# Attention with keys on the partitions, its denominators summed on GpSimd, beside a recurrence whose chunks come first in each step

## The chip, the cores and the metric

The kernel runs on one core of a Trainium2 chip. The metric is the device time of one execution in microseconds; three runs of the kernel before gave 4550.06, 4560.07 and 4565.6, so the median is 4560.07.

## The reference

Two layers of a diffusion transformer on 1024 latent and 256 context tokens of width 1024, all in fp32. In each layer a mixer runs two things side by side: an RWKV-7 recurrence in two directions (8 heads of 64) and an attention (8 heads, queries and keys of 96, values of 64). Latent queries see all 1280 keys, context queries the 256 context keys (first layer only). Input projections come before the mixer, an output projection and a gated FFN with a convolution behind it.

```python
def attend(q, k, v):
    s = jnp.einsum('bqhd,bkhd->bhqk', q, k).astype(F32) * (QK_DIM ** -0.5)
    p = jax.nn.softmax(s, axis=-1).astype(v.dtype)
    return jnp.einsum('bhqk,bkhd->bqhd', p, v)
...
    def step(s, inp):
        r_t, w_t, k_t, v_t, kk_t, a_t = inp
        sa = jnp.einsum('bhvk,bhk->bhv', s, kk_t)
        s = (s * w_t[:, :, None, :]
             - sa[..., None] * (kk_t * a_t)[:, :, None, :]
             + v_t[..., None] * k_t[:, :, None, :])
        return s, jnp.einsum('bhvk,bhk->bhv', s, r_t)
```

## The kernel before

The program is a sequence of stages: input projection (`in_proj`), mixer, output projection (`out_proj`), FFN, once for each layer. A scheduler in the tile framework orders the instructions of each engine from the order of the code and a model of its own, so neighbouring pieces of code end up interleaved on the in-order engines. DMAs are all issued by SyncE (SP).

**Mixer** (`mixer`, L758). Ten steps `i`, each of 128 tokens in each direction. Per step the recurrence has two chunks (`rwkv_seq`, L957: products, the copies `Z` and `W`, then the new state, one half of which is multiplied on VectorE and one on GpSimd, L999, and `S` on GpSimd, L1001); `rwkv_inv2` (L935) ends the inverse of step `i+1`; `rwkv_prep` (L840) prepares step `i+2` and calls `rwkv_inv` (L902). There a loop of 31 turns (L925, L926) solves sixteen small triangular systems with 62 dependent VectorE instructions, each with both inputs in SBUF; it is called **the chain** here. There are 20 chains, ten in each layer. Its tile `T` is set up on GpSimd (L917, L919), and its result is transposed on VectorE into `X` by four instructions (L932). In the code of a step the attention of that step comes first, then the two chunks.

**Attention** (`attn`, L1037), one call for a pair of heads and 128 queries, 72 calls in all (64 latent, 8 context). Queries are on the partitions: three matmuls for each key segment (high and low parts of a split in two, L1075) give scores in three PSUM tiles `sp`; VectorE takes the least of each (L1076) and joins them (L1085); ScalarE makes `exp(least - score)` and its row sums (L1088); VectorE joins the sums (L1095) and inverts them (L1096). Then 128x128 pieces of `P` are transposed on TensorE (L1107), copied out of PSUM by VectorE and ScalarE in turn (L1110, L1112) and multiplied by the values (L1117). The inverse sums are spread over partitions by a product with the identity (L1120), copied (L1122) and multiplied in (L1123).

**Behind the mixer.** When the last inverse is done, its SBUF is given to the output projection's weights: `split_wo` (L748) loads 16 pieces of 256 KB into a tile `raw` with two buffers, and splits each on ScalarE (L755) and VectorE (L756). The first products of `out_proj` are those of L1228.

```python
for j in range(31):
    r, w = 31 - j, j // 2 + 1
    tmp = p.tile([128, 152], F32, name="tmp", tag="tmp")
    tv = tmp[:, :r * w].rearrange("p (a b) -> p a b", b=w)
    eng.tensor_tensor(tv, bc(Dt[:, j + 1:, j:j + 1], [128, r, w]), bc(T[:, j:j + 1, :w], [128, r, w]), op=ALU.mult)
    eng.tensor_tensor(T[:, j + 1:, :w], T[:, j + 1:, :w], tv, op=ALU.subtract)
```

Of the kernel before, what the change touches and what calls it, by code (L numbers as in the profile page):

```python
# [22 lines left out]
NP = 4  # L23
# [8 lines left out]
CUTS = [(0,), (1,), (2,)]  # L32
# [41 lines left out]
def bc(ap, shape):  # L74
    return ap.to_broadcast(shape)
# [6 lines left out]
class Kern:  # L82
# [654 lines left out]
    def load_wo(self, l, st):  # L737

        nc = self.nc
        wp = st.enter_context(self.tc.tile_pool(name=f"ow{l}", bufs=1, side="right", reuse_waits="tile"))  # L740
        self.wo = [None] * 8
        for k in range(7, -1, -1):
            self.wo[k] = [wp.tile([128, D], F32R, name=f"{nm}{k}") for nm in ("lo", "hi")][::-1]
        with self.tc.tile_pool(name=f"or{l}", bufs=2, side="right", reuse_waits="tile") as p:
            for k in range(8):
                self.split_wo(l, k, p, "raw")
# [11 lines left out]
    def mixer(self, l, wst):  # L758
        tc = self.tc
        with ExitStack() as st:  # L760
# [6 lines left out]
            order = ([8, 9] if need_ctx else []) + [3, 4, 2, 5, 1, 6, 0, 7]  # L767
            work = [(h, t) for h in range(NP) for t in order]
# [4 lines left out]
            for i in range(10):  # L773

                upto = len(work) * (i + 1) // 10 if i < 9 else len(work)
                for h, t in work[done:upto]:
                    self.attn(l, h, t, t == order[0])
                done = upto
                self.rwkv_seq(l, i, 0)
                self.rwkv_seq(l, i, 1)  # L780
# [121 lines left out]
    def rwkv_inv(self, l, i, AB):  # L902
# [26 lines left out]
        X = R.X[i % 2]  # L929
        for j in range(4):  # L930
            r = slice(32 * j, 32 * j + 32)
            nc.vector.transpose(X[r, :, 32 * (j % 2):32 * (j % 2) + 32], TD[r])  # L932
        R.inv = (AB, TD)

    def rwkv_inv2(self, l, i):  # L935
# [19 lines left out]
        nc.vector.tensor_copy(X[64:96, :, 32:64], ps[64:96])  # L955

    def rwkv_seq(self, l, i, c):  # L957
# [21 lines left out]
        nc.vector.tensor_copy(Z, ps)  # L979
# [49 lines left out]
    def attn_setup(self, l, st):  # L1029
        tc = self.tc  # L1030
        A = self.A = Ctx()
        A.n = 0
        A.p = st.enter_context(tc.tile_pool(name=f"A{l}", bufs=1, reuse_waits="tile"))
        A.ps = st.enter_context(tc.tile_pool(name=f"As{l}", bufs=1, space=PSUM, reuse_waits="tile"))
        A.pp = st.enter_context(tc.tile_pool(name=f"Ap{l}", bufs=1, space=PSUM, reuse_waits="tile"))

    def attn(self, l, h, t, first):  # L1037

        nc = self.nc
        A = self.A  # L1040
        p = A.p
        if first:
            A.k = []
            for e in range(2):
                raw = p.tile([128, NTOK], F32, name="raw", tag="P", bufs=3)[0:96]
                nc.sync.dma_start(out=raw[0:64], in_=self.kD[l][2 * h + e])
                nc.sync.dma_start(out=raw[64:96], in_=self.krD[l])
                k = p.tile([96, 2, NTOK], F32R, name="ka", tag=f"ka{e}")
                nc.scalar.activation(k[:, 0], raw, AF.Copy)
                nc.vector.tensor_tensor(k[:, 1], raw, k[:, 0], op=ALU.subtract)  # L1050
                A.k.append(k)
            A.v = p.tile([128, NTOK // 128, 128], F32, name="va", tag="va")
            nc.sync.dma_start(out=A.v, in_=self.vD[l][:, :, h * 128:(h + 1) * 128].rearrange("t p x -> p t x"))
        raw = p.tile([96, 2, 128], F32, name="qr", tag="qr", bufs=2)
        nc.sync.dma_start(out=raw, in_=self.qD[l][2 * h:2 * h + 2, :, t * 128:(t + 1) * 128].rearrange("h r t -> r h t"))
        q = p.tile([96, 2, 2, 128], F32R, name="qa", tag="qa", bufs=2)
        nc.scalar.activation(q[:, 0], raw, AF.Copy)
        nc.gpsimd.tensor_tensor(q[:, 1], raw, q[:, 0], op=ALU.subtract)
        key_segs = SEGS if t < 8 else SEGS[2:]
        k0 = key_segs[0][0]  # L1060
        nk = NTOK - k0
        Ps, dn = [], []
        for e in range(2):
            mx = p.tile([128, 12], F32, name="mx", tag="mx", bufs=6)
            P = p.tile([128, NTOK], F32, name="P", tag="P", bufs=3)
            cut = CUTS if t < 8 else [(2,)]
            sps = []
            for i, c in enumerate(cut):
                sp = A.ps.tile([128, 512 * max(len(x) for x in CUTS[i:i + 1])], F32, name="sp", tag=f"s{i}")
                b0 = SEGS[c[0]][0]  # L1070
                w = sum(SEGS[x][1] for x in c)
                for x in c:
                    o, n = SEGS[x]
                    for m, (qq, kk) in enumerate(((0, 0), (0, 1), (1, 0))):
                        nc.tensor.matmul(sp[:, o - b0:o - b0 + n], q[:, qq, e], A.k[e][:, kk, o:o + n], start=m == 0, stop=m == 2)  # L1075
                nc.vector.tensor_reduce(mx[:, i:i + 1], sp[:, :w], axis=AX.X, op=ALU.min)  # L1076
                sps.append((sp, b0 - k0, w))
            nx = len(cut)
            mn = mx[:, 0:1]
            if nx > 1:  # L1080
                mn = mx[:, 8:9]
                if nx == 2:
                    nc.vector.tensor_tensor(mn, mx[:, 0:1], mx[:, 1:2], op=ALU.min)
                else:
                    nc.vector.tensor_reduce(mn, mx[:, 0:nx], axis=AX.X, op=ALU.min)  # L1085

            for i, (sp, o, w) in enumerate(sps):
                nc.scalar.activation(P[:, o:o + w], sp[:, :w], AF.Exp, bias=mn, scale=-1.0, accum_out=mx[:, 4 + i:5 + i])  # L1088
            sm = mx[:, 4:5]
            if nx > 1:  # L1090
                sm = mx[:, 9:10]
                if nx == 2:
                    nc.vector.tensor_tensor(sm, mx[:, 4:5], mx[:, 5:6], op=ALU.add)
                else:
                    nc.vector.tensor_reduce(sm, mx[:, 4:4 + nx], axis=AX.X, op=ALU.add)  # L1095
            nc.vector.reciprocal(mx[:, 3:4], sm)  # L1096
            Ps.append(P)
            dn.append(mx[:, 3:4])
        av = A.pp.tile([128, 512], F32, name="av", tag="av")
        half = [slice(0, 64), slice(64, 128)]  # L1100
        nkt = nk // 128
        for kp in range(nkt // 2):
            tp = A.pp.tile([128, 2, 2, 128], F32, name="tp", tag="tp", bufs=1)
            for e in range(2):
                for b in range(2):
                    o = (kp * 2 + b) * 128
                    nc.tensor.transpose(tp[:, b, e], Ps[e][:, o:o + 128], self.ident)  # L1107
            pT = p.tile([128, 2, 2, 128], F32, name="pT", tag="pT", bufs=2)
            if A.n % 2:
                nc.scalar.activation(pT, tp, AF.Copy)  # L1110
            else:
                nc.vector.tensor_copy(pT, tp)  # L1112
            A.n += 1
            for b in range(2):
                kt = kp * 2 + b
                for e in range(2):
                    nc.tensor.matmul(av[half[e], 0:128], A.v[:, k0 // 128 + kt, half[e]], pT[:, b, e], start=kt == 0, stop=kt == nkt - 1)  # L1117

        for e in range(2):
            nc.tensor.matmul(av[half[e], 128:256], bc(dn[e], [128, 64]), self.ident, start=True, stop=True)  # L1120
        o1 = p.tile([128, 128], F32, name="o1", tag="o1", bufs=2)
# [346 lines left out]
```

## Time and profile before

| | |
|---|---|
| median of three runs | 4560.07 us |
| profiled execution | 4568.71 us, span 4566.9 us |
| TensorE busy | 4159.5 us (91%) |
| VectorE busy | 2736.5 us (60%) |
| ScalarE busy | 1688.5 us (37%) |
| GpSimd busy | 541.9 us (12%) |
| granted TensorE clock | 0.938 of full speed |

The profiled execution is 8.6 us above the median. Busy shares are means over stages with different limits: the mixers run from about 690 to 1420 us and from about 3018 to 3705 us of the span, and what the change touches is almost all in there. The busy time of an engine is the union of its instructions' records; TensorE's records overlap each other, because matmuls are pipelined.

### The profile page before, as it was taken

The page shows a single profiled execution, that of the slowest core. Times are in us where ns is not written, and L with a number is a line of the kernel's source. Part 1 is how long each engine was busy: PE and PEld are TensorE (multiplying, and loading weights), DVE is VectorE, ACT ScalarE, POOL GpSimd, SP SyncE. Part 2 cuts the span into 40 slices and gives each one's busy share as a digit, 9 for nine tenths or more (in the row PEclk, how much of TensorE's full clock was granted, in tenths as well). Part 3 has the DMA queues.
Part 4 walks back from the last instruction along what each step waited for, and adds up shares of the span by engine and source line. Part 5 has one row for each costly group of instructions (what it writes and reads, how often), then busy time and mean ns, then how long its engine had stood idle before and what let it go on. Part 6 is the DMA issues. An engine that isn't in the chain of part 4 may idle for free. (4 is left out here: it accounts for less than half of the span.)

```text
span 4566.9 us, 72983 instructions
## 1 busy us (share of the span) xinstructions
PE 4159.5 (91%) x29598; PEld 3294.7 (72%) x29598; DVE 2736.5 (60%) x4943; ACT 1688.5 (37%) x3000; POOL 541.9 (12%) x492
## 2 busy tenths in 40 slices
PE   8978888888888899999998989988889878999998
PEld 5756656676766788888886866666777666888887
DVE  3225567888885534554447235569887866555456
ACT  3213455444554432221224224454445534222222
POOL 1000000111222300000004000001111244000002
PEclk9998889899998999999998998989998989999999
DMA  6652234323324211111113222343232243111111
GB/s 222 237 180 91 104 120 125 84 69 81 79 61 140 100 37 35 40 42 33 47 35 111 84 71 100 117 144 77 61 81 66 65 136 126 54 51 51 44 50 65
DMA packets 425698, 401.36 MB, mean 88 GB/s; under 512 B 243473, under 2 KB 329937, under 8 KB 425361
## 3 DMA queue, kind: packets, MB, share of 16 engines
q1 hardware_dynamic: 425360, 396.69, 28.1%
q8 instruction: 233, 3.82, 0.3%
q14 instruction: 105, 0.85, 0.1%
HBM read 285.85 MB, written 110.72 MB: 87 GB/s over the span
## 5 line engine op out<-in xcount | busy, mean ns | idle before, releaser
L1279 PE MATMUL up<-u,hi 128*128 128x512 f32 (+1 forms) x3520 | 1012.6, 369 | 4.2 <-ACT hi L1269 4.2
L1279 PEld LDWEIGHTS up<-u,hi 128*128 128x128 f32 x3520 | 643.8, 189 | 119.8 <-ACT hi L1269 4.6
L1279 PE MATMUL up<-u,lo 128*128 128x512 f32 (+1 forms) x1760 | 648.5, 368 | 0.0
L304 PE MATMUL pj<-u,whi 128*128 128x512 f32 (+1 forms) x1888 | 567.2, 385 | 36.0 <-DVE o L325 31.0
L1326 DVE TENSOR_TENSOR acc<-dn,acc 128x512 f32<-128x512 f32 x340 | 233.3, 688 | 432.9 <-PE dn L1320 432.8
L304 PEld LDWEIGHTS pj<-u,whi 128*128 128x128 f32 x1888 | 352.6, 198 | 139.4 <-issue 45.2
L1279 PEld LDWEIGHTS up<-u,lo 128*128 128x128 f32 x1760 | 332.1, 189 | 57.9 <-DVE lo L1271 0.3
L304 PE MATMUL pj<-u,wlo 128*128 128x512 f32 (+1 forms) x944 | 360.0, 382 | 0.1
L1075 PE MATMUL sp<-ka,qa 96*128 96x512 f32 (+1 forms) x1200 | 320.8, 399 | 37.2 <-ACT P L1088 26.1
L1269 ACT ACTIVATE hi<-raw 128x512 fp32r<-128x512 f32 x176 | 110.5, 630 | 564.4 <-PE up L1279 561.4
L1320 PE MATMUL dn<-hi,fh 128*128 128x512 f32 x792 | 311.8, 394 | 7.9 <-ACT fh L1294 4.0
L1320 PE MATMUL dn<-lo,fh 128*128 128x512 f32 x792 | 310.0, 391 | 0.0
L1320 PE MATMUL dn<-hi,fl 128*128 128x512 f32 x792 | 305.9, 390 | 0.0
L1088 ACT ACTIVATE P<-sp,mx 128x512 f32<-128x512 f32 (+1 forms) x400 | 240.0, 607 | 174.1 <-DVE mx L1085 98.4
L1117 PE MATMUL av<-pT,va 128*64 128x128 f32 x2624 | 235.5, 302 | 51.3 <-DVE pT L1112 25.5
L1075 PEld LDWEIGHTS sp<-ka,qa 96*128 96x128 f32 x1200 | 214.8, 205 | 89.6 <-ACT P L1088 38.5
L1107 PE MATMUL tp<-cst,P 128*128 128x128 f32 x1312 | 236.7, 303 | 22.5 <-ACT P L1088 16.4
L1076 DVE TENSOR_REDUCE mx<-sp 128x1 f32<-128x512 f32 (+1 forms) x400 | 229.4, 586 | 39.7 <-PE sp L1075 37.1
L1117 PEld LDWEIGHTS av<-pT,va 128*64 128x64 f32 x2624 | 152.0, 146 | 108.6 <-DVE pT L1112 31.7
L1271 DVE TENSOR_TENSOR lo<-raw,hi 128x512 fp32r<-128x512 f32 x176 | 125.4, 715 | 173.8 <-ACT hi L1269 161.3
L287 ACT ACTIVATE whi<-raw 128x512 fp32r<-128x512 f32 (+2 forms) x110 | 66.1, 602 | 435.7 <-PE pj L304 384.5
L304 PEld LDWEIGHTS pj<-u,wlo 128*128 128x128 f32 x944 | 186.6, 198 | 39.2 <-issue 7.3
(254 smaller groups left out, 7233.5 us busy)
## 6 DMA issues: line engine op xcount, KB each, us to landing
wt<-in_w_ada_dram SPq DMA_DIRECT2D x96, 512.0 KB
raw<-in_w_up_dram SPq DMA_DIRECT2D x176, 256.0 KB
raw<-in_w_down_dram SPq DMA_DIRECT2D x88, 256.0 KB
raw<-in_w_in_dram SPq DMA_DIRECT2D x84, 256.0 KB
bkD<-lt SPq DMA_DIRECT2D x32, 640.0 KB
BK<-bkD SPq DMA_DIRECT2D x320, 64.0 KB
KR<-kkD SPq DMA_DIRECT2D x152, 128.0 KB
kkD<-kx SPq DMA_DIRECT2D x16, 640.0 KB
```

What stands on the lines that cost most here:

```text
L287: nc.scalar.activation(hi[:, :m], raw[:, :m], AF.Copy)
L304: nc.tensor.matmul(ps[:, o:o + n], ww, u[k][s], start=k == 0 and j == 0, stop=k == nk - 1 and j == 2)
L1075: nc.tensor.matmul(sp[:, o - b0:o - b0 + n], q[:, qq, e], A.k[e][:, kk, o:o + n], start=m == 0, stop=m == 2)
L1076: nc.vector.tensor_reduce(mx[:, i:i + 1], sp[:, :w], axis=AX.X, op=ALU.min)
L1088: nc.scalar.activation(P[:, o:o + w], sp[:, :w], AF.Exp, bias=mn, scale=-1.0, accum_out=mx[:, 4 + i:5 + i])
L1107: nc.tensor.transpose(tp[:, b, e], Ps[e][:, o:o + 128], self.ident)
L1117: nc.tensor.matmul(av[half[e], 0:128], A.v[:, k0 // 128 + kt, half[e]], pT[:, b, e], start=kt == 0, stop=kt == nkt - 1)
L1269: nc.scalar.activation(hi, raw, AF.Copy)
L1271: nc.vector.tensor_tensor(lo, raw, hi, op=ALU.subtract)
L1279: nc.tensor.matmul(ps[:, so:so + sn], ww, uu[k][s], start=k == 0 and m == 0, stop=k == 7 and m == 2)
L1320: nc.tensor.matmul(ps, x[:, t * 128:(t + 1) * 128], w, start=m == 0, stop=m == 3 * len(js) - 1)
L1326: nc.vector.tensor_tensor(dst, ps, dst, op=ALU.add)
```

## The change

Attention is written anew, and four pieces around it are moved.

- A call now takes a pair of heads and 256 queries (36 units: 32 latent, 4 context). First, ahead of its use, the least score of each query is found from the high parts alone: one matmul where the scores take three (`least`), reduced on VectorE. Four small products put these on a row, which ScalarE copies into row 96 of the queries (`row`); row 96 of the keys is -1, so that the scores come out with the least already taken off.
- Scores have the keys on the partitions, 128 keys by 2 heads by 256 queries, six matmuls. ScalarE makes the exponentials straight into the form in which the products with the values need them: no transposes, no copies.
- GpSimd sums the exponentials over the ten key tiles (nine additions of 128x512 for a unit; 292 in all). At the end a product with ones sums over the partitions, and VectorE inverts 128x256 sums and multiplies.
- A unit is cut into steps of two key tiles; the steps of a layer are shared out among the ten steps of the mixer, and in the code each chunk of the recurrence comes before its half of the attention's steps.
- `X` comes from one transpose of 128x512 on VectorE and four copies on ScalarE; the copies `Z` and the second half of L954/L955 go to ScalarE.
- `raw` of the output projection's weights has one buffer in place of two; a scratch tile of `out_proj` is wider.

```diff
-        with self.tc.tile_pool(name=f"or{l}", bufs=2, side="right", reuse_waits="tile") as p:
+        with self.tc.tile_pool(name=f"or{l}", bufs=1, side="right", reuse_waits="tile") as p:
...
-                for h, t in work[done:upto]:
-                    self.attn(l, h, t, t == order[0])
+                self.rwkv_seq(l, i, 0)
+                for step in work[done:(done + upto) // 2]:
+                    step()
+                self.rwkv_seq(l, i, 1)
+                for step in work[(done + upto) // 2:upto]:
+                    step()
                 done = upto
-                self.rwkv_seq(l, i, 0)
-                self.rwkv_seq(l, i, 1)
...
+        Xt = p.tile([128, 16, 32], F32, name="Xt", tag="Xt")
+        nc.vector.transpose(Xt.rearrange("p u s -> p (u s)"), TD.rearrange("p u s -> p (u s)"))
         for j in range(4):
             r = slice(32 * j, 32 * j + 32)
-            nc.vector.transpose(X[r, :, 32 * (j % 2):32 * (j % 2) + 32], TD[r])
+            nc.scalar.activation(X[r, :, 32 * (j % 2):32 * (j % 2) + 32], Xt[r], AF.Copy)
...
-        nc.vector.tensor_copy(X[64:96, :, 32:64], ps[64:96])
+        nc.scalar.activation(X[64:96, :, 32:64], ps[64:96], AF.Copy)
...
-        nc.vector.tensor_copy(Z, ps)
+        nc.scalar.activation(Z, ps, AF.Copy)
...
+        def least(t):
...
+            def product(out, e, o, n):
+                nc.tensor.matmul(out, q[0:96, 0, e, tok], A.k[e][0:96, 0, o:o + n], start=True, stop=True)
...
+                for e in range(2):
+                    for i in range(2):
+                        sp = pp.tile([128, 512], F32, name="sp", tag="s", bufs=4)
+                        product(sp, e, 512 * i, 512)
+                        nc.vector.tensor_reduce(mx[:, e, i:i + 1], sp, axis=AX.X, op=ALU.min)
...
+        def scores(kt):
+            q = c["q"]
+            st = pp.tile([128, 2, 256], F32, name="st", tag="s", bufs=4)
+            ks = slice(kt * 128, (kt + 1) * 128)
             for e in range(2):
...
+                k = A.k[e]
+                nc.tensor.matmul(st[:, e], k[0:97, 0, ks], q[0:97, 0, e], start=True, stop=False)
+                nc.tensor.matmul(st[:, e], k[0:96, 0, ks], q[0:96, 1, e], start=False, stop=False)
+                nc.tensor.matmul(st[:, e], k[0:96, 1, ks], q[0:96, 0, e], start=False, stop=True)
+
+            P = c[kt] = p.tile([128, 2, 256], F32, name="P", tag="P", bufs=6)
+            nc.scalar.activation(P, st, AF.Exp, scale=-1.0)
+            if kt == kts[1]:
+                c["sum"] = p.tile([128, 2, 256], F32, name="Ps", tag="Ps")
+                nc.gpsimd.tensor_tensor(c["sum"], c[kts[0]], P, op=ALU.add)
+            elif kt > kts[1]:
+                nc.gpsimd.tensor_tensor(c["sum"], c["sum"], P, op=ALU.add)
...
+                nc.tensor.matmul(c["av"][half[e], 0], A.v[:, kt, half[e]], c[kt][:, e], start=kt == kts[0], stop=kt == kts[-1])
+
+        def close():
+
+            av = c["av"]
+            ones = bc(self.cst[:, CO_ONE:CO_ONE + 1], [128, 64])
+            for e in range(2):
+                nc.tensor.matmul(av[half[e], 1], ones, c["sum"][:, e], start=True, stop=True)
...
+            nc.vector.reciprocal(of, av[:, 1])
+            nc.vector.tensor_tensor(of, av[:, 0], of, op=ALU.mult)
...
+        def tiles(i):
+            for kt in kts[2 * i:2 * i + 2]:
+                scores(kt)
+            for kt in kts[2 * i - 2:2 * i] if i else []:
+                values(kt)
+            if 2 * i == len(kts):
+                close()
```

How the built programs stand. First VectorE in the first layer, where the fifth chain ends (`T` is the chain's tile, `Dt` its matrix; `KR` and `GA` belong to the preparation of the step after the next). Before, then after:

```order
L1123 TENSOR_TENSOR o_8939<-av,o_8939 128x128
L1112 COPY pT<-tp 128x512
L925 TENSOR_TENSOR tmp<-Dt,T 128x30
L1076 TENSOR_REDUCE mx<-sp 128x1
L926 TENSOR_TENSOR T<-T,tmp 128x2x15
L887 TENSOR_TENSOR KR<-g,cst 64x4x64
L890 TENSOR_TENSOR GA<-g,cst 128x256
L1085 TENSOR_REDUCE mx<-mx 128x1
L925 TENSOR_TENSOR tmp<-Dt,T 128x16
L926 TENSOR_TENSOR T<-T,tmp 128x16
L928 STREAM_TRANSPOSE TD<-T 128x32x16
L932 STREAM_TRANSPOSE X_4537<-TD 32x16x32 x4
```

```order
L925 TENSOR_TENSOR tmp_7517<-Dt_7427,T_7429 128x45
L926 TENSOR_TENSOR T_7429<-T_7429,tmp_7517 128x3x15
L925 TENSOR_TENSOR tmp_7520<-Dt_7427,T_7429 128x30
L926 TENSOR_TENSOR T_7429<-T_7429,tmp_7520 128x2x15
L925 TENSOR_TENSOR tmp_7523<-Dt_7427,T_7429 128x16
L887 TENSOR_TENSOR KR_8131<-g_8150,cst_60 64x4x64
L890 TENSOR_TENSOR GA_8148<-g_8150,cst_60 128x256
L926 TENSOR_TENSOR T_7429<-T_7429,tmp_7523 128x16
L887 TENSOR_TENSOR KR_8131<-g_8151,cst_60 64x4x64
L890 TENSOR_TENSOR GA_8148<-g_8151,cst_60 128x256
L928 STREAM_TRANSPOSE TD_7526<-T_7429 128x32x16
L931 STREAM_TRANSPOSE Xt_7528<-TD_7526 128x512
```

Between the turns of the chain stood pieces of the attention at nearly every place; now its last turns follow each other, with only the preparation between them, and one transpose of 512 columns stands for four.

Then GpSimd from the setting up of `T` for the fifth chain on, in the first layer (`W` and `S` are the recurrence's, `qa` the low parts of the queries, `Ps` the attention's sums). Before, then after:

```order
L917 MEMSET T_7651 128x512
L919 TENSOR_SCALAR T_7651<-cst_60 128x16 x2
L1058 TENSOR_TENSOR qa_8945<-qr_8943,qa_8945 96x256
L999 TENSOR_TENSOR W_6642<-St_8261,pc0_91 64x512
L1001 TENSOR_TENSOR S_8265<-St_8261,pc0_91 128x512
L1058 TENSOR_TENSOR qa_9058<-qr_9056,qa_9058 96x256
```

```order
L917 MEMSET T 128x512
L919 TENSOR_SCALAR T<-cst 128x16 x2
L1137 TENSOR_TENSOR Ps<-Ps,P 128x512 x4
L1135 TENSOR_TENSOR Ps<-P 128x512
L1137 TENSOR_TENSOR Ps<-Ps,P 128x512 x4
L1001 TENSOR_TENSOR W<-St,pc_91 64x512
L1003 TENSOR_TENSOR S<-St,pc_91 128x512
L1137 TENSOR_TENSOR Ps<-Ps,P 128x512 x4
```

The queue that held a handful of the recurrence's instructions for each step now holds the attention's sums between them, nine ahead of the first `W`.

Last ScalarE at the end of the first mixer, where the output projection's weights begin (`hi` are their high parts). Before, then after:

```order
L954 ACTIVATE X_4538<-p_13070 32x16x32
L755 ACTIVATE hi_13124<-raw 128x512 x2
L1110 ACTIVATE pT<-tp 128x512
L755 ACTIVATE hi_13122<-raw 128x512 x2
L985 ACTIVATE W<-q 64x512
L1088 ACTIVATE P,mx<-sp,mx 128x512 x2
```

```order
L956 ACTIVATE X_4539<-p_12269 32x16x32
L957 ACTIVATE X_4539<-p_12269 32x16x32
L754 ACTIVATE hi_12323<-raw 128x512
L981 ACTIVATE Z<-q 128x512
L754 ACTIVATE hi_12323<-raw 128x512
L987 ACTIVATE W<-q 64x512
```

The attention's exponentials, which went on beside the weights before, are all ahead of them now; beside the weights only the recurrence's last chunks are left.

## Rows read from the trace of the kernel before

**Rows 1.** Windows (us; busy of PE, PEld, DVE, ACT, POOL; clock, DMA): mixers, steady stretches.

```profile
690.00:1420.00 730.00, 629.04 (x8079) 493.93 (x8078) 584.03 (x1528) 376.38 (x872) 123.57 (x139) 0.92 0.33 86
3018.00:3705.00 687.00, 595.30 (x7636) 469.74 (x7634) 555.78 (x1460) 342.73 (x799) 110.70 (x125) 0.91 0.31 78
...
786.40:1347.10 560.70, 490.96 (x6808) 388.70 (x6807) 478.32 (x1268) 284.02 (x663) 103.32 (x116) 0.94 0.30 74
3098.30:3640.00 541.70, 478.05 (x6490) 378.95 (x6490) 466.47 (x1239) 266.10 (x621) 92.15 (x105) 0.93 0.28 70
```

**Rows 2.** TensorE in order of time, 1101 to 1103 us: start, length, what.

```profile
1101.81 0.66 PE L1117 MATMUL av<-pT,va 128*64 128x128 f32 x8
1102.30 0.39 PE L1120 MATMUL av<-cst,mx 128*64 128x128 f32 x4
1102.61 0.66 PE L1107 MATMUL tp<-cst,P 128*128 128x128 f32 x4
1103.03 0.95 PE L1075 MATMUL sp<-ka,qa 96*128 96x512 f32 x3
```

**Rows 3.** VectorE, then GpSimd, in order of time inside the tenth chain.

```profile
1311.10 0.68 DVE L996 TENSOR_TENSOR St<-q,S 128x512 f32<-128x512 f32 x1
1311.70 0.27 DVE L925 TENSOR_TENSOR tmp<-Dt,T 128x115 f32<-128x115 f32 x1
...
1313.44 1.11 DVE L926 TENSOR_TENSOR T<-T,tmp 128x115 f32<-128x115 f32 x1
...
1313.05 1.37 POOL L1001 TENSOR_TENSOR S<-St,pc 128x512 f32<-128x512 f32 x1
```

**Rows 4.** Groups by line and form, VectorE: count, busy us, mean ns, idle before.

```profile
L1076 DVE TENSOR_REDUCE mx<-sp 128x1 f32<-128x512 f32 x256 | 174.0, 683 | 37.8 <-PE sp L1075 35.5
L1076 DVE TENSOR_REDUCE mx<-sp 128x1 f32<-128x256 f32 x144 | 59.6, 414 | 1.9 <-PE sp L1075 1.6
L1112 DVE COPY pT<-tp 128x512 f32<-128x512 f32 x164 | 112.1, 684 | 29.0 <-PE tp L1107 27.6
L1085 DVE TENSOR_REDUCE mx<-mx 128x1 f32<-128x3 f32 x128 | 18.9, 148 | 0.8
L1096 DVE RECIPROCAL mx<-mx 128x1 f32<-128x1 f32 x144 | 22.2, 154 | 4.1 <-ACT P L1088 3.3
L1123 DVE TENSOR_TENSOR o<-av,o 128x128 f32<-128x128 f32 x72 | 20.2, 281 | 12.1 <-ACT o L1122 11.6 <-DMA BK<-bkD 0.3
L932 DVE STREAM_TRANSPOSE X<-TD 32x512 f32<-32x512 f32 x80 | 56.1, 701 | 1.1
L620 DVE TENSOR_TENSOR_SCAN lt<-rst,lt 128x640 f32<-128x640 f32 x32 | 45.9, 1475 | 11.5 <-issue 9.8 <-ACT lt L618 1.7
```

**Rows 5.** Groups by line: the chain's two lines, and a GpSimd addition of 128x512.

```profile
L926 DVE TENSOR_TENSOR T<-T,tmp 128x126 f32<-128x126 f32 (+22 forms) x620 | 198.2, 320 | 10.9
L925 DVE TENSOR_TENSOR tmp<-Dt,T 128x126 f32<-128x126 f32 (+22 forms) x620 | 185.1, 299 | 10.1
L834 POOL TENSOR_TENSOR ysb<-ysb,bo 128x512 f32<-128x512 f32 x18 | 23.0, 1277 | 110.7 <-DVE ysb L833 87.3 <-DVE mx L1096 16.1 <-DVE T L926 7.3
```

**Rows 6.** The chain's lines by themselves: least, median and longest ns, first and last start.

```profile
L925 DVE TENSOR_TENSOR tmp<-Dt,T x620: 154/264/1244, 745.8 to 3637.3; 128x126 f32<-128x126 f32 x15, 128x30 f32<-128x30 f32 x10, 128x78 f32<-128x78 f32 x10, 128x110 f32<-128x110 f32 x10
L926 DVE TENSOR_TENSOR T<-T,tmp x620: 147/267/1823, 746.5 to 3639.8; 128x126 f32<-128x126 f32 x15, 128x30 f32<-128x30 f32 x10, 128x78 f32<-128x78 f32 x10, 128x110 f32<-128x110 f32 x10
```

**Rows 7.** Waits: GpSimd, us in total, times, longest.

```profile
POOL W L999 <- DVE St L996: 187.1, 22, 23.2
```

**Rows 8.** Second mixer's end in order of time, and the output projection's first products.

```profile
3651.86 1.29 DVE L756 TENSOR_TENSOR lo<-raw,hi 128x512 fp32r<-128x512 f32 x2
3652.58 6.58 SPq L754 DMA_DIRECT2D raw<-in_w_o_dram  x4
3655.72 1.24 ACT L755 ACTIVATE hi<-raw 128x512 fp32r<-128x512 f32 x2 [1.14 <-DMA raw<-in_w_o_dram]
...
L1228 PE MATMUL ps<-hi,mh x128: 390/397/796, 3707.8 to 3810.9; 128*128 128x512 f32 x128
```

More of the change, by code (lines that the diff above doesn't have):

```diff
@@ L31 @@
 SEGS = [(0, 512), (512, 512), (1024, 256)]
-CUTS = [(0,), (1,), (2,)]
 PV_CONV = 0
@@ L766, in mixer @@
             need_ctx = l < DEPTH - 1
-            order = ([8, 9] if need_ctx else []) + [3, 4, 2, 5, 1, 6, 0, 7]
-            work = [(h, t) for h in range(NP) for t in order]
+            work = self.attn_work(l)
             done = 0
@@ L1031, in attn_setup @@
         A = self.A = Ctx()
-        A.n = 0
         A.p = st.enter_context(tc.tile_pool(name=f"A{l}", bufs=1, reuse_waits="tile"))
-        A.ps = st.enter_context(tc.tile_pool(name=f"As{l}", bufs=1, space=PSUM, reuse_waits="tile"))
         A.pp = st.enter_context(tc.tile_pool(name=f"Ap{l}", bufs=1, space=PSUM, reuse_waits="tile"))
[L1037 to L1043, printed above, removed]
-            for e in range(2):
[L1045 to L1103, printed above, removed]
-            for e in range(2):
[L1105 to L1121, printed above, removed]
-        nc.scalar.activation(o1, av[:, 128:256], AF.Copy)
-        nc.vector.tensor_tensor(o1, av[:, 0:128], o1, op=ALU.mult)
-        nc.sync.dma_start(out=self.mixD[l][t, :, 4 + h], in_=o1)
@@ new lines, in attn_setup, with attn_work @@
+        A.k = [A.p.tile([97, 2, NTOK], F32R, name=f"ka{e}") for e in range(2)]
+        for e in range(2):
+            self.nc.scalar.activation(A.k[e][96:97, 0], bc(self.cst[96:97, CO_ONE:CO_ONE + 1], [1, NTOK]), AF.Copy, scale=-1.0)
+    def attn_work(self, l):
+        groups = ([4] if l < DEPTH - 1 else []) + [1, 2, 0, 3]
+        work = []
+        for h in range(NP):
+            units = [self.attn(l, h, g) for g in groups]
+            work.append(lambda h=h: self.attn_keys(l, h))
+            work += units[0][0]
+            for u, (_, tiles) in enumerate(units):
+                ahead = units[u + 1][0] if u + 1 < len(units) else []
+                mixed = [((i + 0.5) / len(v), j, f) for j, v in enumerate((tiles, ahead)) for i, f in enumerate(v)]
+                work += [f for _, _, f in sorted(mixed, key=lambda x: x[:2])]
+        return work
@@ new lines, in attn_keys @@
+    def attn_keys(self, l, h):
+        nc, A = self.nc, self.A
+        for e in range(2):
+            raw = A.p.tile([96, NTOK], F32, name="raw", tag="raw", bufs=1)
+            nc.sync.dma_start(out=raw[0:64], in_=self.kD[l][2 * h + e])
+            nc.sync.dma_start(out=raw[64:96], in_=self.krD[l])
+            k = A.k[e]
+            nc.scalar.activation(k[0:96, 0], raw, AF.Copy)
+            nc.vector.tensor_tensor(k[0:96, 1], raw, k[0:96, 0], op=ALU.subtract)
+        A.v = A.p.tile([128, NTOK // 128, 128], F32, name="va", tag="va")
+        nc.sync.dma_start(out=A.v, in_=self.vD[l][:, :, h * 128:(h + 1) * 128].rearrange("t p x -> p t x"))
@@ L1195, in out_proj @@
             g0 = p.tile([128, D], F32, name="gate", tag="gate", bufs=1)
-            sp = p.tile([128, 872], F32, name="uf", tag="uf", bufs=1)
+            sp = p.tile([128, 1592], F32, name="uf", tag="uf", bufs=1)
             m0 = p.tile([128, 8, 128], F32, name="m", tag="m")
@@ L1204, in out_proj @@
             uf = [sp]
[L1205 removed]
+            ufs = lambda: (uf.pop() if uf else p.tile([128, 1592], F32, name="uf", tag="uf", bufs=1))[:, :512].rearrange(
                 "p (j t) -> p j t", j=4)
```

45 lines of the change are left out of this document (44 added, 1 removed).

## The prediction

> **What bounds the kernel now.** I read the stretches of the mixers first, because the page's chain of waits ends in the FFN and tells nothing of them. The two mixers, 730 and 687 us, hold nearly all that the change touches [rows 1]. Inside them I take the part from the first chain's end to the last one's, where all pieces run beside each other: VectorE is busy for 478.3 of 560.7 us and 466.5 of 541.7, 85 and 86%; TensorE shows 88% in both; ScalarE 51 and 49%; GpSimd 18 and 17% [rows 1]. TensorE's share is too high to be read as its load: eight value products are recorded with 0.66 us, but the next group starts after 0.49, and four transposes with 0.66 where the next starts after 0.42 [rows 2]. By the ratio of about 0.7 its real occupation is near 61%. VectorE's records overlap much less: one of 0.68 us, and the next starts after 0.60 [rows 3]. So VectorE bounds the mixer, and a microsecond taken off its queue is worth 0.60 / 0.68 = 0.88 us of the time. The rest of its stretch is idle: 82.4 + 75.2 = 157.6 us.
>
> **VectorE: what goes.** The reductions of the scores, 174.0 + 59.6 = 233.6 us; half of the copies of transposed pieces, 112.1; the joins, 18.9, and as much again for the same instruction on the sums, 37.8; the small reciprocals, 22.2; the final products, 20.2; the four transposes of `X`, 56.1 [rows 4]. Sixty copies (forty of `Z`, twenty of the second half of `X`) go to ScalarE, at the 0.684 us of a copy of 512 columns [rows 4]: 41.1. Together 523.1 us.
>
> **VectorE: what comes.** 328 reductions of 512 columns (ten for each of 32 latent units, two for each of four context units) at 0.683: 224.0. 64 joins at 0.148: 9.5. Twenty transposes of 512 columns at 0.701: 14.0. 36 final products of 256 columns, at the 0.414 of a reduction of 256: 14.9 [rows 4]. Then 36 reciprocals of 128x256, a shape that the trace does not show. Low end: the scan's 1475 / 640 = 2.3 ns a column [rows 4], 0.59 us. High end: the reciprocal's own row, 154 ns for one column [rows 4]. A reduction grows by (683 - 414) / 256 = 1.05 ns a column, so that its 148 ns for three columns hold 145 that are no column's, and the reciprocal's one column costs 9 ns: 0.145 + 256 x 0.009 = 2.4 us. I take the high end, since it is the only row of that operation: 86.4 us, against 21.2 at the low one. Together 348.8, and net VectorE loses 174.3 us.
>
> The Trainium skill ("VectorE: DVE Perf Modes", "First, the fixed hardware budget") has Reciprocal as an iterative divide with a repeat count of 8. Eight passes at the 0.269 us that 256 columns cost in a reduction would be about 2.3 us, an estimate by that page, and the sum would come out 3 us lower.
>
> **GpSimd's sums and the chain.** 292 additions of 128x512 at 1.277 us [rows 5] are 373 us. GpSimd goes from 234 us in the mixers [rows 1] to about 607 of 1417, so it does not become the bound by its load. But it costs VectorE something. While GpSimd ran `S` from 1313.05 for 1.37 us, a chain instruction that usually takes about 0.27 took 1.11, and it ended (1314.55) only after that one (1314.42) [rows 3]. The chain's two lines take 0.299 and 0.320 us in the mean [rows 5] and 0.264 and 0.267 in the median [rows 6]; 620 times the difference is 54.6 us, which I put on the 103.3 + 92.2 = 195.5 us of GpSimd's work in the steady stretches [rows 1]: 0.28 us of stall for each. For the sums: 373 x 0.28 = 104 us, or 0.36 us a sum. Low end 0 (the sums fall where VectorE reads PSUM). High end: every sum holds one instruction by the full 1.11 - 0.27 = 0.84 [rows 3], 245 us. I take 104. VectorE's net is then -174.3 + 104 = -70, and by 0.88, **-62 us**.
>
> **The close of a unit.** The product with ones waits for the last sum, and behind it on TensorE's queue stand the next scores, which VectorE's reductions need. The last sum takes 1.28 us after its exponential, and four value products of 256 columns, as eight of 128, cover 0.49 of it [rows 2, 5]: 0.79 us, 36 times, **+28 us**. Ends: 0 (other pieces stand between), and two sums in the queue, 2.07 us each, 74. GpSimd is in order, and its `W` waits for `St` 22 times, 187.1 us, once for 23.2 [rows 7]; sums behind it come late. Six buffers of `P` cover six tiles of that, so I add nothing; it is what lies behind the high end.
>
> **Edits at nothing.** TensorE loses 1312 transposes (four in 0.42 us: 138 us) and 72 groups of four denominators (0.31 us each: 22), and gets a third product for the least scores (three scores products in 0.95 us, 328 of them: 104), 144 row products (11) and 72 of ones (11) [rows 2]: -34 us beside a VectorE that ends the waits. Were TensorE the bound, this too would be a gain. ScalarE gets 80 + 60 copies and loses as many pieces of the transposes as VectorE did, 164 [rows 4]; it was half idle [rows 1].
>
> **The end of the mixer.** The weights' loads wait for the last inverse. With one buffer each load of four DMAs (issued at 3652.58) is followed by the split (3655.72), and the next may start when `lo` is done (3651.86 with 1.29 us for two) [rows 8]: about 3.1 + 0.6 + 0.4 = 4.1 us a piece, 16 pieces 66 us, after some 12 us from the chain's end (3639.8 [rows 6]) to the first. Before, the first output product came at 3707.8 [rows 8], 68 us behind that end, and now it would come after about 78, of which the attention, which is ahead of the weights now, gives back some 10. Nothing, give or take 10 us in each mixer.
>
> **Sum.** -62 + 28 = -34 us, on the profiled execution's 4568.7, is 4534.7. That execution is 8.6 above the median, so the forecast is **4526 us** against 4560.
>
> **The rivals.**
>
> *A, slower: each sum holds VectorE for most of its length.* The one place looked at shows it: the instruction ended 0.13 us after GpSimd's [rows 3]. For it: attention no longer puts PSUM reads between all turns of the chain, so a turn meets a sum more often. Against: the mean over both mixers is 0.28 us for each us [rows 1, 5, 6]. At 0.84 a sum: -174.3 + 245 = +71, by 0.88 +62, and +28: +90, **4650 us**. It decides from the point where (-174.3 + 292 s) x 0.88 + 28 is zero: s = 0.49 us, not far above the 0.36 that I took. The Trainium skill ("SBUF — State Buffer", "Who interferes with whom") says it as a rule: VectorE with two SBUF inputs and a GpSimd instruction that reads SBUF exclude each other for the whole instruction. By that rule this rival is right wherever the two meet; the row inside the tenth chain agrees.
>
> *B, the reciprocal is cheap.* At 0.59 us, 36 x 1.81 = 65 us less, by 0.88 57: **4469 us**. For it: a full-width scan needs only 2.3 ns a column; against it: its own row, though 9 ns are little to read from.
>
> *C, the idle stretches fill.* VectorE idles 157.6 us of the steady stretches [rows 1], mostly between chains, where it waits for the recurrence's products on TensorE. Chunks now come first in a step, and the least scores are independent of them. Half of it filled: 79 us more, **4447 us**. Against: nothing in the rows says that the next chain starts earlier; it needs the inverse's and the preparation's turns all the same.
>
> That the change does not do what it says is excluded by the order of the built program.
>
> **How the numbers follow.** 0.3% is 13.7 us, about what a measurement tells from no change: 4546 to 4574. Forecast 0.40 (own range 4480 to 4560: the reciprocal's and the close's low ends below, some of the stall's above; 0.07 of it within 0.3%), A 0.23 (0.04 of it within, 0.19 slower), B 0.15, C 0.22. Faster 0.33 + 0.15 + 0.22 = 0.70, same 0.11, slower 0.19. The range, 4405 to 4610, leaves out B with C together (4390) and the far half of A.
>
> **What the profile after would show.** The reductions of the least scores at 0.68 us, 328 times. The reciprocal at 2.4 us (forecast) or 0.6 (B). The chain's lines: means of about 0.299 + 104 / 1240 = 0.38 and 0.40 us for the forecast, near 0.5 for A, unchanged where the sums cost nothing. GpSimd near 600 us in the mixers, its additions at 1.28 us or longer by VectorE's hold. Waits of the ones product on GpSimd of about 28 us. From chain to chain some 61 us before (1102.4 us for 18 steps); 59 for the forecast, below 56 for C, 65 for A. The last chain's end to the first output product: 68 us, give or take 10. What would make it wrong: TensorE in fact the bound, so that its 34 us count and VectorE's stalls don't; or the sums so late behind `W` that `P` runs out of buffers and the scores stop.

## The result, and the profile after

The changed kernel takes 4766.32 us (median of 4 runs, 4761.35 to 4785.41), the kernel before 4556.4 beside it: a ratio of 1.0467, 95% interval 1.0432 to 1.0502. It is 4.7% slower, outside the range, on the side of rival A and beyond its price.

The profiled execution has a span of 4764.6 us, 197.7 longer. The same two windows as in [rows 1], from the first chain's end to the last one's, in the changed kernel:

```profile
796.80:1423.20 626.40, 522.09 (x6417) 403.59 (x6413) 508.91 (x992) 262.94 (x448) 257.43 (x222) 0.87 0.26 64
3201.90:3821.30 619.40, 523.40 (x6056) 406.25 (x6053) 483.90 (x972) 246.71 (x423) 238.85 (x209) 0.81 0.24 59
```

They grew from 1102.4 to 1245.8 us, 69.2 us a step after 61.2. VectorE is busy for 992.8 us (944.8 before), but idle for 253.0 (157.6). The rest of the 197.7 us lies around them: the first input projection ends 6.3 us later, the first chains end 4.1 and 16.5 us later behind the input projections' last products, the two tails are 3.4 and 8.7 us longer, the two output projections 6.4 and 9.1.

I cut the steady stretches once more, by adding up windows: the eighteen in which a chain runs, and the eighteen from one chain's end to the next one's start. e1 is the first experiment below: the changed kernel without GpSimd's sums. These two numbers carry most of what follows.

| | chain runs, us | between chains, us | VectorE busy in the two |
|---|---|---|---|
| before | 735.8 | 366.6 | 667.8, 277.0 |
| changed | 752.7 | 493.0 | 705.5, 287.2 |
| e1, without sums | 630.6 | 475.9 | 572.2, 264.6 |

So there are two changes in one: the sums lengthen the stretches with a chain by 122 us and the others by 17 (e1 to changed), and all the rest of the change shortens the first by 105 and lengthens the others by 109 (before to e1).

Groups by line of the changed kernel, in answer to [rows 4, 5]: the least scores, the reciprocal, the one transpose of `X`, the chain, the sums.

```profile
L1102 DVE TENSOR_REDUCE mx<-sp 128x1 f32<-128x512 f32 x256 | 164.7, 678 | 36.2 <-PE sp L1093 35.9
L1153 DVE RECIPROCAL o<-av 128x256 f32<-128x256 f32 x36 | 63.0, 1750 | 12.0 <-PE av L1150 11.7
L931 DVE STREAM_TRANSPOSE Xt<-TD 128x512 f32<-128x512 f32 x20 | 14.1, 705 | 0.5
L925 DVE TENSOR_TENSOR tmp<-Dt,T 128x126 f32<-128x126 f32 (+22 forms) x620 | 280.2, 452 | 16.8
L926 DVE TENSOR_TENSOR T<-T,tmp 128x126 f32<-128x126 f32 (+22 forms) x620 | 278.3, 449 | 17.6
L1137 POOL TENSOR_TENSOR Ps<-Ps,P 128x512 f32<-128x512 f32 x256 | 329.8, 1288 | 302.4 <-ACT P L1132 278.8
```

The chain's two lines went from 383.3 to 558.5 us, 175 more. The sums themselves are no longer than priced (1.288 us). How the two meet is seen in order of time inside the ninth chain, GpSimd first (two of the sums, `Ps`, and two other instructions of its queue), then VectorE:

```profile
1297.74 1.27 POOL L1137 TENSOR_TENSOR Ps<-Ps,P 128x512 f32<-128x512 f32 x1 [11.00 <-ACT P L1132]
1298.96 1.26 POOL L834 TENSOR_TENSOR ysb<-ysb,bo 128x512 f32<-128x512 f32 x1
1300.18 1.27 POOL L1083 TENSOR_TENSOR qa<-qr,qa 96x512 fp32r<-96x512 f32 x1
1301.40 1.29 POOL L1137 TENSOR_TENSOR Ps<-Ps,P 128x512 f32<-128x512 f32 x1
```

```profile
1297.61 0.20 DVE L926 TENSOR_TENSOR T<-T,tmp 128x30 f32<-128x30 f32 x1
1297.85 1.24 DVE L925 TENSOR_TENSOR tmp<-Dt,T 128x58 f32<-128x58 f32 x1
1299.12 1.18 DVE L926 TENSOR_TENSOR T<-T,tmp 128x58 f32<-128x58 f32 x1
1300.33 1.24 DVE L925 TENSOR_TENSOR tmp<-Dt,T 128x56 f32<-128x56 f32 x1
1301.61 1.16 DVE L926 TENSOR_TENSOR T<-T,tmp 128x56 f32<-128x56 f32 x1
```

Each of the last four chain instructions ends 0.08 to 0.12 us after one of GpSimd's has ended, and the chain makes one step for each of these, at 1.2 us in place of 0.22 (the median of the same forms, before and after). Of the chain's 1240 instructions, 52 took over 1 us before the change and 231 after it. All 231 overlap a two-input instruction of GpSimd, and 229 of them end within 0.2 us of the end of one; before the change all 52 do both.

Of the 143 us by which the steady stretches grew, 48 are busy time of VectorE and 95 idle. VectorE's waits over the second steady stretch, before and then changed (us in total, times, longest), show where most of the idle time stands: the preparation of a later step (`KR`) waits for TensorE's products far longer (in the first stretch 13.9 us before and 54.1 changed).

```profile
DVE KR L887 <- PE g L884: 17.8, 24, 1.8
```

```profile
DVE KR L887 <- PE g L884: 68.0, 32, 6.0
```

### The profile page after: what moved, and what is told of

Its sections match the earlier page's. It is cut to its first block, busy times and chain, and to the rows that moved or that the text cites. A ratio compares the mean times of both kernels' runs of the same rounds, so it can differ in the third digit from the quotient of the medians.

```text
span 4764.6 us, 69422 instructions
## 1 busy us (share of the span) xinstructions
PE 4221.0 (89%) x28286; PEld 3318.8 (70%) x28286; DVE 2773.6 (58%) x4259; ACT 1626.3 (34%) x2436; POOL 906.2 (19%) x748
## 5 line engine op out<-in xcount | busy, mean ns | idle before, releaser
L1137 POOL TENSOR_TENSOR Ps<-Ps,P 128x512 f32<-128x512 f32 x256 | 329.8, 1288 | 302.4 <-ACT P L1132 278.8
L925 DVE TENSOR_TENSOR tmp<-Dt,T 128x126 f32<-128x126 f32 (+22 forms) x620 | 280.2, 452 | 16.8
L926 DVE TENSOR_TENSOR T<-T,tmp 128x126 f32<-128x126 f32 (+22 forms) x620 | 278.3, 449 | 17.6
L1132 ACT ACTIVATE P<-st 128x512 f32<-128x512 f32 x328 | 191.5, 596 | 271.1 <-PE st L1129 247.8
L1127 PE MATMUL st<-qa,ka 97*128 97x256 f32 x656 | 218.6, 333 | 10.3 <-DVE mx L1102 5.6
L1143 PE MATMUL av<-P,va 128*64 128x256 f32 x1312 | 214.0, 424 | 12.3 <-DVE o L1154 9.6
L1128 PE MATMUL st<-qa,ka 96*128 96x256 f32 x656 | 205.7, 314 | 0.0
```

The source lines that it names most:

```text
L1127: nc.tensor.matmul(st[:, e], k[0:97, 0, ks], q[0:97, 0, e], start=True, stop=False)
L1128: nc.tensor.matmul(st[:, e], k[0:96, 0, ks], q[0:96, 1, e], start=False, stop=False)
L1132: nc.scalar.activation(P, st, AF.Exp, scale=-1.0)
L1137: nc.gpsimd.tensor_tensor(c["sum"], c["sum"], P, op=ALU.add)
L1143: nc.tensor.matmul(c["av"][half[e], 0], A.v[:, kt, half[e]], c[kt][:, e], start=kt == kts[0], stop=kt == kts[-1])
```

## The experiments

All ratios are to the kernel before, run beside them; in brackets the 95% interval.

**Are the sums what holds VectorE?** e1 takes them out:

```diff
-                nc.gpsimd.tensor_tensor(c["sum"], c["sum"], P, op=ALU.add)
...
-                nc.tensor.matmul(av[half[e], 1], ones, c["sum"][:, e], start=True, stop=True)
+                    nc.tensor.matmul(av[half[e], 1, t * 128:(t + 1) * 128], ones, self.ident, start=True, stop=True)
```

> Leaves out the sums of the exponentials: the 292 GpSimd additions are gone and the product with ones reads the identity, so that the division is by 1. All else as in the changed kernel, order included. Theory H (GpSimd's sums hold the chain's instructions on VectorE): the chain's two lines took 558.5 us in the changed kernel and 383.3 in the one before; they go back to means of 0.30 to 0.32 us and the time falls by the 175 us or more, to 4590 or below (ratio to before 1.00 to 1.01). Theory O (the new order of chunks and attention leaves VectorE idle between the chains: 253 us idle in the steady stretches against 158): the stall was only filling time in which VectorE would have waited, the time falls by less than 100, to 4670 or more. Theory C (copies on ScalarE lengthen the recurrence's path): as O, 4670 or more.

1.0097 (1.0063 to 1.0132); the chain's lines are back at 0.311 and 0.305 us:

```profile
L925 DVE TENSOR_TENSOR tmp<-Dt,T 128x126 f32<-128x126 f32 (+22 forms) x620 | 193.1, 311 | 16.7 <-DVE T L926 0.2
L926 DVE TENSOR_TENSOR T<-T,tmp 128x126 f32<-128x126 f32 (+22 forms) x620 | 189.0, 305 | 16.5
```

The ratio is at the upper end of H's range, and H holds: of the 4.7%, 3.7 are the sums. But the other 1% stays, with VectorE busy for 836.8 us in the steady stretches, 108 less than before:

```profile
811.10:1373.10 562.00, 504.72 (x6448) 397.96 (x6446) 420.56 (x988) 261.51 (x447) 97.53 (x99) 0.87 0.29 72
3136.00:3680.40 544.40, 475.03 (x6098) 373.41 (x6096) 416.28 (x964) 246.47 (x423) 87.75 (x90) 0.88 0.27 67
```

These stretches are 1106.4 us long, 4 more than before the change, so the 1% does not lie in them. Of the 54 us by which the profiled execution's span exceeds that of the kernel before, the first chains behind the input projections have 27 and the output projections 20. No run tried the cause of either (in e4, which runs nearly the changed kernel's order, the second layer's first chain ends 11 us later than in the changed kernel, so single executions differ here by about that much).

f3 keeps GpSimd's queue as full, but reads only one column of each tile from SBUF:

```diff
-                nc.gpsimd.tensor_tensor(c["sum"], c["sum"], P, op=ALU.add)
+                nc.gpsimd.tensor_copy(d[:, 0:1], P[:, 0, 0:1])
+                nc.gpsimd.memset(d[:, 1:], 0.0)
+                nc.gpsimd.memset(d[:, 1:], 0.0)
```

> In place of each sum GpSimd copies one column of the exponentials, which makes it wait for them, and then fills a tile twice (2 x 0.53 us and about 0.1, as long as a sum): the queue is as full as in the changed kernel, but next to nothing is read from SBUF. The denominators are left out as in e1. Theory H (an addition that reads SBUF holds VectorE's chain instructions): the chain's lines near 0.31 us, the time that of e1 within 25 us, ratio 1.005 to 1.015. Theory Q (the full queue is what costs: W and S of the recurrence and the buffers of the exponentials come late): as the changed kernel, ratio 1.035 to 1.05.

1.0189 (1.0147 to 1.023): below Q's range, above H's. In its groups by line the stand-ins occupy GpSimd for 153 + 153 + 62 = 368 us, about as long as the sums (376), and as much of it beside the chains (GpSimd is busy there for 322 us, in the changed kernel for 330). The chain is not held by them, its lines take what they take in e1:

```profile
L1137 POOL MEMSET Ps<- 128x511 f32 x292 | 153.0, 524 | 11.6
L1136 POOL MEMSET Ps<- 128x511 f32 x292 | 153.0, 524 | 583.2 <-PE pj L303 570.4
L1135 POOL COPY Ps<-P 128x1 f32<-128x1 f32 x292 | 61.6, 211 | 459.0 <-ACT P L1132 454.6
```

```profile
L926 DVE TENSOR_TENSOR T<-T,tmp 128x126 f32<-128x126 f32 (+22 forms) x620 | 194.8, 314 | 16.7
L925 DVE TENSOR_TENSOR tmp<-Dt,T 128x126 f32<-128x126 f32 (+22 forms) x620 | 188.4, 304 | 16.0
```

So the hold comes with the additions, which read two SBUF tiles, and neither from a busy GpSimd nor from its writes, which the memsets make too. Some 0.9% (f3 less e1) is left for the full queue.

f7 sums only the first head (`c["sum"][:, 0]`, 256 columns):

> The 292 sums stay on GpSimd, but only over the first head, 256 columns in place of 512; the second head is divided by the first one's sums. Theory H with a hold by the length of the addition: half of the 146 us that lie between e1 and the changed kernel, ratio 1.023 to 1.034, the chain's lines near 0.38 us. A hold by the instruction, whatever its length: ratio 1.038 or more, the chain's lines at 0.42 us or more.

1.018 (1.0143 to 1.0216), lower than either forecast: an addition takes 0.754 us, the chain's lines 0.362 and 0.363 us. Half the width costs 38% of the hold (67.6 of 176.4 us) and 22% of the time.

e3 puts the additions on VectorE (`nc.gpsimd` becomes `nc.vector`):

> The 292 sums move from GpSimd to VectorE, 512 columns each, some 0.69 us: 201 us of VectorE work in place of the hold of about 175 us. Theory H: the chain's lines back to 0.31 us, the time about the changed kernel's, ratio 1.035 to 1.06. Theory L: the additions fill VectorE's idle time between the chains, the time that of e1 plus 50 at most, ratio 1.010 to 1.021.

1.0372 (1.0331 to 1.0412): the chain back to 0.309 and 0.294 us, the additions 178.2 + 24.7 us. H's range; a sum costs about the same on either engine, 0.69 us of VectorE's time there, and 0.60 on GpSimd by its hold (176.4 / 292).

**Can TensorE sum?** e6 sets 64 columns of ones beside a head's 64 values; e2 multiplies each tile with ones into a PSUM tile of its own.

```diff
-                nc.tensor.matmul(c["av"][half[e], 0], A.v[:, kt, half[e]], c[kt][:, e], start=kt == kts[0], stop=kt == kts[-1])
+                nc.tensor.matmul(c["av"][e], A.v[:, kt, e], c[kt][:, e], start=kt == kts[0], stop=kt == kts[-1])
...
+                nc.scalar.activation(of[half[e]], av[e][half[1 - e]], AF.Copy)
```

> The sums are taken by TensorE for nothing: 64 columns of ones stand beside the values of a head, so that the value products give the sums on the other 64 partitions; ScalarE moves them across, VectorE inverts and multiplies in two halves. No additions on GpSimd, no product with ones. Three score buffers in place of four and four P buffers in place of six pay for the space. VectorE gets 36 more products of 0.41 us, 15 us. Theory H: the chain's lines at 0.30 to 0.32 us, the time as without sums plus about 15: 4605 or below. Theories O and C: 4670 or more.

> The sums are taken by TensorE: a product with ones for each key tile and head, added up in a PSUM tile of its own (three score buffers in place of four), 656 products of 256 columns at 0.22 us, 142 us more of TensorE work less the 72 closing products; none on GpSimd. Theory K (in e1 TensorE is less dense, its granted clock falls from 0.93 to 0.88 in the steady stretches, and the groups of products on the recurrence's path run at the lower level): the clock comes back to 0.91 or more, the time at e1's ratio of 1.010 or below. Theory T (TensorE's load): ratio 1.025 to 1.04.

e6 1.0124 (1.0095 to 1.0154), 55 us above the kernel before and some 24 above H's bound; e2 1.017 (1.0135 to 1.0205), between the ranges of K and T. Both compute the reference's attention without the hold, and both stay above the kernel before. In e2 the clock came back (0.91 and 0.93 in the steady stretches) and the time did not. That speaks against K, the lower clock, as the main cause of what e1 leaves, though e2 also has more work on TensorE and one score buffer less, so it doesn't close the matter.

**Order and copies.** e4 puts the attention's pieces ahead of both chunks in the code; e5 puts the copies back on VectorE in the changed kernel; h5 does so without sums; f4 gives the copies to the kernel before.

```diff
-            nc.vector.transpose(X[r, :, 32 * (j % 2):32 * (j % 2) + 32], TD[r])
+            nc.scalar.activation(X[r, :, 32 * (j % 2):32 * (j % 2) + 32], Xt[r], AF.Copy)
...
-        nc.vector.tensor_copy(Z, ps)
+        nc.scalar.activation(Z, ps, AF.Copy)
```

> Only the order is undone: in each step all of the attention's pieces first, then both chunks, as before the change; the sums stay on GpSimd. Theory H: the chain's lines stay at about 0.45 us and the time within 40 us of the changed kernel's 4766. Theory O: VectorE's idle time in the steady stretches goes back towards 158 us, the time falls by 95 us, to 4670. Theory C: 4766 within 20.

> Only the copies go back to VectorE: Z, the second half of X, and X by four transposes in place of one and four ScalarE copies. VectorE gets 41 us of copies and 42 us of transposes more. Theory H: these copies read PSUM, the chain's stall stays; time 4766 to 4840. Theory C: the chunks' path gets shorter by the ScalarE queue's waits, the time falls by 40 us or more, to 4725 or below. Theory O: 4766 to 4840.

> The kernel without sums (e1), and the copies back on VectorE (Z, X by four transposes, its second half): what the new attention alone does, its sums apart. The copies alone gained 0.5% on the kernel before (0.9951). If the parts add up, ratio 1.010 to 1.020; if VectorE's load does not matter beside the new attention, 1.006 to 1.012; above 1.025 if it does.

> The kernel before the change with only the copies of the change: X by one VectorE transpose of 128x512 and four ScalarE copies, Z and the second half of X on ScalarE. VectorE loses 56.1 - 14.0 + 41.1 = 83 us. Theory V: the time falls by 0.88 x 83 = 73 us, ratio 0.984. Theory T: these pieces stand between the chains, where VectorE waits for TensorE; ratio 0.996 to 1.004.

e4: 1.0435 (1.0407 to 1.0463). The scheduler built nearly the same order from this code (in the traces ScalarE's and GpSimd's instructions follow each other as in the changed kernel, one pair on VectorE and two on TensorE have changed places), so it is a second run of the changed kernel and says nothing on O; it does say that "chunks first" in the code reaches the chip as nothing. e5: 1.0485 (1.0448 to 1.0521), not apart from the changed kernel, so C is not borne out. h5: 1.016 (1.0131 to 1.0189), and f4: **0.9951 (0.9929 to 0.9974), faster than both kernels**. In the old attention the copies gain 0.5%; beside the new one without sums it is 0.6% (h5 less e1, whose intervals all but touch), and beside the sums nothing that stands apart (e5). The new attention by itself, with the rest of the change, costs 1.6% even with its sums left out. V (VectorE bounds the mixer all through, as the prediction had it) had asked 0.984 of f4, T 0.996 or more; f4's VectorE lost 73.5 us of busy time in the steady stretches for 39.1 us of length.

**What bounds, then?** f1 leaves VectorE's reciprocal out of e1, f2 one of TensorE's three score products, f5 all of the attention; h3 keeps of the attention only the loads and TensorE's products.

```diff
-            nc.vector.reciprocal(of, av[:, 1])
-            nc.vector.tensor_tensor(of, av[:, 0], of, op=ALU.mult)
+            nc.vector.tensor_copy(of, av[:, 0])
```

> The kernel without sums (e1), and also without the reciprocal of 128x256: the values are copied out undivided. VectorE loses 36 x 1.75 = 63 us, nothing else changes. Theory V (VectorE bounds the mixer all through, as the prediction had it): the time falls by 0.88 x 63 = 55 us against e1, to a ratio of 0.998 to before. Theory T (VectorE bounds only while a chain runs; between the chains TensorE does, busy 445 of 476 us there in e1, so that work taken off VectorE only lets the stretches between the chains grow): within 25 us of e1, ratio 1.004 to 1.013.

> The kernel without sums (e1), and also without the second of the three score products (the low parts of the queries are left out): TensorE loses 656 products of 256 columns, 656 x 0.118 = 77 us at the full clock; VectorE, ScalarE and GpSimd keep their work. Theory V: within 15 us of e1, ratio 1.006 to 1.013. Theory T: the time falls by 35 us (the share that stands between the chains) to 80 us, ratio 0.992 to 1.002.

> All of the attention is left out; each unit only writes a constant block, so that the recurrence runs alone in the mixer, in the changed kernel's form. Theory L (a serial path of the recurrence through TensorE, ScalarE and VectorE sets the step, so that taking 63 us off VectorE or 77 us off TensorE gave nearly nothing): the steady stretches, 61 us a step before the change and in e1, stay at 48 us a step or more; the time 4340 or more. Theory U (the loads of the engines add up in turn, VectorE's while a chain runs and TensorE's between the chains): the step falls to about 35 us, little over the 30 us that VectorE works in it for the recurrence; the time near 4100.

> The attention is cut to what TensorE and the loads do: the least, score, value and ones products run on a constant in place of the exponentials; no reductions, no exponentials, no sums, no reciprocals; the row products are left out. VectorE and GpSimd work for the recurrence alone, as in the kernel without attention (49.7 us a step, TensorE's clock 0.59 to 0.68 of full speed). Theory L (the recurrence's own path sets the step): within 5 us of 49.7 a step, the time 4250 to 4430, and if the lower clock lengthened that path, below 49.7. Theory T (TensorE's queue, with attention's products between those of the path): 57 us a step or more, the time 4470 or more.

f1: 1.007 (1.0047 to 1.0093), where V asked for 0.998. The stretches with a chain shrank by 52.5 us and the others grew by 38.4. f2: 1.0116 (1.0075 to 1.0158), no gain, so TensorE's load alone is not the bound either: in its steady stretches TensorE was busy for 897 us after 980 in e1, and they were 12 us shorter; the clock there fell to 0.85 and 0.83. f5 and h3 (two runs each), their steady stretches:

```profile
763.40:1217.40 454.00, 288.18 (x4590) 247.60 (x4590) 302.58 (x790) 160.19 (x273) 76.38 (x81) 0.65 0.28 68
2951.90:3391.80 439.90, 287.01 (x4426) 248.34 (x4426) 300.39 (x786) 149.78 (x260) 72.85 (x78) 0.62 0.26 63
```

```profile
779.10:1306.00 526.90, 461.85 (x6159) 378.17 (x6157) 315.31 (x797) 182.24 (x309) 95.61 (x96) 0.88 0.30 75
3055.60:3560.20 504.60, 438.31 (x5959) 357.51 (x5957) 317.06 (x794) 173.20 (x298) 88.27 (x90) 0.90 0.29 73
```

The recurrence alone needs 49.7 us a step (4338.77 us, 1.2 below the bound of L, by which the recurrence's own path sets the step), with VectorE busy for two thirds of it and TensorE at a granted clock of 0.65 and 0.62. With TensorE's attention products in the queue it is 57.3 (4513.35 us), T's side, though VectorE does nothing for the attention there but the low parts of the keys. In the kernel before, with all of its attention, it was 61.2. By this measure, which holds for the changed kernel's products in the order that was built, savings on VectorE, ScalarE and GpSimd together could hardly have been worth much more than 4 us a step.

**A last try on f4**: more of the copies of transposed pieces on ScalarE, all of them (h1, `if True:` for `if A.n % 2:`) or two of three (h2, `if A.n % 3:`).

> The kernel before with the change's copies (f4), and all of the copies of transposed pieces on ScalarE in place of every second one: VectorE loses another 164 x 0.684 = 112 us, most of it while a chain runs, ScalarE gets 164 x 0.6 = 98 us. Theory V or its form for the chains alone (VectorE bounds while a chain runs, busy 632 of 705 us there in f4): the time falls by 50 to 98 us, ratio 0.975 to 0.984. Theory L: the stretches between the chains grow by as much as the chains shrink, ratio 0.992 to 1.000.

> The same with two of three copies of transposed pieces on ScalarE: VectorE loses 55 x 0.684 = 37 us against f4. Theory V: ratio 0.986 to 0.990. Theory L: within 0.4% of f4, 0.991 to 0.999.

1.0032 (1.0016 to 1.0048) and 1.0003 (0.9982 to 1.0024), both above f4 and a little above the ranges of V and L. In h1 the stretches with a chain fell from 704.6 to 622.4 us and those between grew from 358.6 to 458.2. It is the trade of e1 again, in the old attention; besides, the first tail was 22.6 us longer than in f4.

## Why the prediction was wrong, point by point

- **"VectorE bounds the mixer, and a microsecond taken off its queue is worth 0.88"** failed. The 174.3 us of savings stand in the sum as -153; without the sums (e1) the kernel was 46 us slower than before. The step holds only while a chain runs: there VectorE is busy for 91% [before, table above], and e1, f1 and h1 each shortened these stretches. The work that no longer fits beside the chain, TensorE's products and the recurrence's preparation, then stands between the chains, in a path from engine to engine (products, copies, products), where VectorE waits. Before the change VectorE spent 45 us on the preparation beside chains and 62 between them; in e1 20 and 86. Of the 108 us that VectorE's busy time lost in e1, the steady stretches gave back none. That the move of the preparation is the cause of the longer stretches is argued from this shift; no run moved it alone, and e3 speaks against it as the whole cause: there the preparation stood as before (42 and 65 us), and the stretches between the chains took 455 us all the same. What the slower kernels share is more of the recurrence's products on TensorE between the chains (182 us before, 252 in e1, 255 in e3, 265 in the changed kernel); that may be the cause or the effect. The prediction's own sign of being wrong, TensorE as the bound, came nearer: with its attention products alone the step was 57.3 of 61.2 us (h3), though fewer of them gained nothing (f2).
- **The hold, "0.28 us for each us" of GpSimd, 0.36 a sum** was mis-sized: 176 us, 0.60 a sum, after 104 and 0.36. In time it was 3.7%, some 169 us, where the sum has 92. The mean over the old kernel's mixers spreads the few meetings over all of GpSimd's work, and the single row, 0.84 [rows 3], takes every sum for such a meeting; 0.60 lies about halfway, and beyond the 0.49 from which rival A decides. A was right in its mechanism and short in its price (+90 us against +210), because it too credited VectorE's other savings in full.
- By the rule of the Trainium skill ("SBUF — State Buffer", "Who interferes with whom") a VectorE instruction with two SBUF inputs and a GpSimd instruction that reads SBUF exclude each other for the whole instruction. The rows of the ninth chain agree, and so does f3, whose memsets read nothing.
- **The reciprocal**: 1.750 us, between the ends of 0.59 and 2.4; 23 us less than taken. B and C did not come: the idle time grew in place of being filled.
- **The close**: TensorE's product with ones waited for GpSimd's sums twice, for 5.8 us in all, against 28.
- **GpSimd's load** was right (603 us in the mixers against 607), as were the least reductions (0.68) and the end of the mixer (75.0 and 76.5 us from the last chain to the first output product, forecast 68 give or take 10). Not foreseen was that the output projections themselves take 6 and 9 us longer; their cause was not tried.
- **TensorE "at nothing"**: its clock was not in the sum. It fell from 0.94 and 0.93 to 0.87 and 0.81 in the steady stretches, TensorE being busy for 84% of them after 88%; e2, where it came back without a gain, speaks against this as the main cause.

## What to carry to other kernels

Before giving GpSimd an elementwise job over SBUF, look at what VectorE does meanwhile: beside a chain of short two-input SBUF instructions each addition here stopped the chain for about half of its own length (0.60 of 1.288 us). An average over all of GpSimd's work priced this too low and a single overlap too high, so look at every long instruction of the chain and at what ran beside it. A high busy share over a window does not make an engine the bound: cut the window by phases first, and take an engine's work out of one phase to see whether the next one grows. When several savings come in one change, run each alone; here the copies were the only part that gained.

## What the runs showed that was not expected

- VectorE and GpSimd can fall into step, one chain instruction for one addition, at about 1.2 us a pair, as long as GpSimd has such additions queued. Halving the additions' length halved neither the hold nor the time, but took 62 and 78% of them away.
- A memset of 128x511 on GpSimd (0.524 us) beside the chain held nothing.
- RECIPROCAL of 128x256 from PSUM takes 1.750 us, some 6.3 ns a column if 0.145 us of it are no column's (an estimate from the reductions of 512 and 256 columns).
- While a chain runs beside the recurrence alone (f5), TensorE is busy for 199 of 441 us and its granted clock is 0.59 of full speed, near the lower of its two levels (1.2 of 2.4 GHz); in the kernel before, busy for 630 of 736 us in these stretches, 0.95, near the upper.
